# Operands at one residue of 256 bytes, and another order at the end of an output projection

## The chip, the core and the metric

The kernel runs on one core of a Trainium2 chip. The core has a matrix engine (TensorE, PE in the profile, with a second row PEld for its weight loads), a vector engine (VectorE, DVE), an activation engine (ScalarE, ACT), a general engine (GpSimd, POOL) and an engine that issues transfers (SyncE, SP). Data lie in SBUF, 128 partitions with one address range per partition, and matrix products land in PSUM. The metric is the device time of one execution in microseconds (us), as the median of several runs.

## The reference

One decoder layer on 1024 tokens of width 1024, all in float32. Two mixers work on the same normalized input, a gated DeltaNet (GDN) with 4 heads of 128 in chunks, and a native sparse attention (NSA) with 8 heads of 64 in 2 groups; their outputs are merged by gates and projected, and a SwiGLU feed-forward network (FFN, hidden width 2816) follows.

```python
h = rms_norm(x, mix_norm_gain)
qkv, z, beta, alpha, q, six K/V of NSA, gates, merge_a, merge_b = split(h @ w_in)
A = gated_delta_net(silu(causal_conv4(qkv)), beta, alpha) * gain * silu(z)
N = native_sparse_attention(q, compressed, selected and window K/V, gates)
merged = sigmoid(merge_a) * (A @ w_branch_gdn) + sigmoid(merge_b) * (N @ w_branch_nsa)
x = x + merged @ w_out
h2 = rms_norm(x, ffn_norm_gain)
gate, up = split(h2 @ w_gate_up)
x = x + (silu(gate) * up) @ w_down
out = rms_norm(x, final_norm_gain)
```

## The kernel before

**Matrix products.** Every large product runs as three matmuls per block (`mmk`, lines 143 to 145): each operand is split into a high part and a remainder by `split` (ScalarE rounds, line 81; DVE subtracts, line 82), and high x high, high x remainder and remainder x high are summed in PSUM. A matmul has a moving operand (here 512, 264 or 256 columns) and a stationary one of 128 columns, which is loaded into the array by PEld. In the timeline's name `pq<-h,whi` the moving operand stands first.

**Stages.** The input is normalized (`rms_scale`, line 156: Square on ScalarE, a scaling on DVE, a power on POOL), transposed and kept as h0 (tokens 0 to 511) and h1 (512 to 1023). Then follow the z projection (8 token tiles, a piece of 264 and a piece of 256 columns), the convolution stage (12 feature tiles; for each one product with h0, then one with h1, 8 blocks of three matmuls each), the chunk loop of GDN, woven by a planner with the projections of NSA (three pieces of 264 and two of 256 columns) and the merge gates (16 feature tiles for each half of the tokens), the attention (also woven with the gates of the second half), the branch products (32 groups of 12 matmuls), the output projection, the FFN and the down projection. In the FFN one level of a Strassen scheme is used: sums and differences of quarters of the activations (called B11, B21, B3 to B7) and of the weights (`quarters`, `left`) go into seven products instead of eight. PE's order is the order of the program; in the chunk loop and in the attention that order comes from `weave`, which asks a model of each stream which of them is ready first. Nothing of the planner's numbers belongs to the change.

**Where tiles lie.** Pools take addresses from the left in the order in which they are opened; some open at the right end (h1, later x1, and the large slots of the branch products, the output projection and the FFN). The constant pool `cp` (line 49) is the first on the left. Small tiles of odd sizes in it and in the pools behind it shift what follows. In the kernel before, the addresses of the main operands have these remainders modulo 256 bytes:

| tiles | address modulo 256 |
|---|---|
| h1, x1, AT, Aop, W, all B tiles, fraw, ahi, alo, sum, act | 224 |
| whi, wlo (split weights until the branch products; stationary for 512 columns, moving for 264 and 256) | 160 |
| h0 | 96 |
| attention: qs, qt, kt | 96 |
| attention: KT, VS, KCS, VCS | 192 |
| gain, ident | 160, 128 |
| c (FFN accumulators), xt of the down projection | 32 |
| zz, th (staging) | 32 and 64 |
| GDN tiles | 0, 32 or 160 |

**End of the output projection.** The product has two column halves. For the second, `o_last(t)` runs token tile t: 8 blocks of three matmuls (two groups kk of four k, `o_mm`), then `o_add` adds the result to x (DVE, line 1298). `h2_scale(i)` starts the norm of tile i (Square on ScalarE, a DVE operation on the sum, a power on POOL, line 162). `h2_rows(i)` finishes it on DVE (line 1329). For i = 4 to 7, `h2_sums(i, ...)` forms the sums number 5, 7, 6 and 4 of the Strassen scheme from tile i and tile i-4, by `psub` on POOL (line 88). `h2_turn(i, n, ...)` transposes such a sum on PE (four 128x128 transposes into one PSUM slot `dn`, of which there are two) and splits it into the B tiles. The argument `then` of `o_last` is a list of calls placed after k = 0, 1, 2, ... of the first group. `prepare(f, n)` splits a quarter of a gate or up weight tile; `product(f, n)` is one Strassen product of 12 matmuls; `f_sums(f)` forms the weight sums on POOL; `f_load(f)` puts the weight loads on SP's queue. From `o_last(4)` on, the order on DVE, ScalarE and POOL is the order of the program too (`manual_schedule`, line 1439), so each call stands in three queues at the place where it is written. For tile 5, for example, the lines are `o_last(5, ...)`, `h2_rows(4)`, `h2_scale(5)`, `h2_sums(4, (5, 7, 6, 4))`: the norm of tile 4 stands on DVE behind the add of tile 5, and the sums of tile 4 stand on POOL behind the power of tile 5.

**GDN tiles.** For each of 8 chunks `prepare_chunks` loads the decay sums E from DRAM (SP), takes sb = exp(E) on ScalarE (line 508), masks E on POOL (lines 510 and 512), multiplies KQ by sb on POOL, copies the last column of sb into `glast` (line 569, DVE), multiplies the products A and qkT by E on DVE (lines 581 and 582), sends A out (SP) and loads blocks of it back as U for a solve of 15 steps on DVE (lines 592 and 594). E and sb have one buffer each, `glast` three. `scan_chunks` has a tile r (DVE) and a tile vn (ScalarE); the product Y r is read into vn.

## Time and profile before

| | before |
|---|---|
| time, median of three runs | 1831.64 us (1830.16 to 1835.03) |
| profiled execution: its own time | 1833.01 us |
| its span in the trace | 1831.3 us |
| PE busy | 1736.3 us, 95% of the span |
| DVE, ACT, POOL busy | 1116.4, 768.0 and 732.7 us |
| mean granted clock of PE over the span | 0.988 of full speed |

All times of the trace count from the start of its span. A row of a timeline tells when an instruction began, how long it took, on which engine and line, out <- in by tile name, the shape, and in brackets how long the engine had been idle before it and which instruction ended that. Matmuls overlap in the pipeline, so the distance between two starts tells more than the duration of one. A granted clock of 1.00 is 2.4 GHz on PE.

### The profile page before, as it was taken

To read this page: it belongs to the slowest core of one execution; us is meant where nothing else is said; L and a number is where in the kernel's file an instruction comes from. 1 tells how busy PE (TensorE), PEld (TensorE's weight loads), DVE (VectorE), ACT (ScalarE), POOL (GpSimd) and SP (SyncE) were. 2 spreads that over 40 slices of the span, in tenths; PEclk is the share of its full clock that TensorE was granted. 3 is DMA by queue.
4 is the path that set the end of the run, shared out by engine and by line. 5 is a ranking of instruction groups with operands and counts; after the bars stand their busy time and mean duration, and the time that the engine had idled before them with its cause. 6 is when DMAs were issued, how large, how long until landed. Compare 5 with 4: busy or idle time off the path is not lost. (4 is left out here: it accounts for less than half of the span.)

```text
span 1831.3 us, 26131 instructions
## 1 busy us (share of the span) xinstructions
PE 1736.3 (95%) x9348; PEld 1459.3 (80%) x9348; DVE 1116.4 (61%) x2014; ACT 768.0 (42%) x1814; POOL 732.7 (40%) x1086
## 2 busy tenths in 40 slices
PE   7999989989999899999999998799999999989998
PEld 7888878988878777877778887588888888867776
DVE  6566466665443687776734434465655556678985
ACT  5244333343221797877722212333333333334352
POOL 3401143353231886665430301544354343354720
PEclk9999999999999999999999999899999999999999
DMA  6322443452463311111077340043233332662242
GB/s 204 98 93 93 140 118 105 107 133 66 135 187 90 94 42 47 25 47 35 13 213 215 105 166 1 19 125 99 92 118 105 106 98 92 220 234 90 83 137 99
DMA packets 183010, 196.40 MB, mean 107 GB/s; under 512 B 23408, under 2 KB 139360, under 8 KB 182880
## 3 DMA queue, kind: packets, MB, share of 16 engines
q1 hardware_dynamic: 164112, 162.03, 29.0%
q0 software_dynamic: 18560, 32.62, 5.9%
q8 instruction: 73, 1.20, 0.3%
q14 instruction: 57, 0.47, 0.1%
q10 hardware_dynamic: 208, 0.09, 0.0%
HBM read 139.01 MB, written 55.69 MB: 106 GB/s over the span
## 5 line engine op out<-in xcount | busy, mean ns | idle before, releaser
L1075 ACT ACTIVATE Ps<-s,mx 128x384 f32<-128x384 f32 (+3 forms) x192 | 106.0, 560 | 23.5 <-DVE mx L1074 22.3
L82 DVE TENSOR_TENSOR ptl<-ppt,pth 128x512 fp32r<-128x512 f32 (+1 forms) x148 | 98.9, 682 | 26.3 <-ACT pth L81 25.7
L81 ACT ACTIVATE ahi<-fraw 128x512 fp32r<-128x512 f32 x88 | 55.5, 632 | 141.4 <-PE M L144 141.4
L1105 POOL TENSOR_SCALAR Ps<-Ps,cs 128x384 f32<-128x384 f32 (+3 forms) x192 | 106.4, 571 | 13.4 <-DVE cs L1083 5.6
L1074 DVE TENSOR_REDUCE mx<-s 128x1 f32<-128x384 f32 (+3 forms) x192 | 94.8, 513 | 19.5 <-PE s L1073 14.0
L1070 PE MATMUL s<-KT,qt 128*128 128x384 f32 (+3 forms) x384 | 100.4, 362 | 2.9 <-DVE ptl L82 1.8
L143 PE MATMUL pn<-whi,h 128*128 128x264 f32 (+1 forms) x320 | 100.2, 313 | 1.4 <-ACT nst L706 1.4
L81 ACT ACTIVATE pth<-ppt 128x512 fp32r<-128x512 f32 (+1 forms) x148 | 87.1, 604 | 26.4 <-PE ppt L1128 24.1
L143 PE MATMUL pm<-h,whi 128*128 128x512 f32 x224 | 97.5, 435 | 0.2 <-ACT thm L721 0.2
L144 PE MATMUL M<-act,ahi 128*128 128x512 f32 x194 | 78.5, 404 | 13.5 <-DVE act L82 13.5
L144 PE MATMUL pn<-wlo,h 128*128 128x264 f32 (+1 forms) x320 | 91.1, 285 | 0.0
L145 PE MATMUL pn<-whi,h 128*128 128x264 f32 (+1 forms) x320 | 91.0, 284 | 0.0
L144 PE MATMUL pm<-h,whi 128*128 128x512 f32 x224 | 89.3, 399 | 0.0
L145 PE MATMUL pm<-h,wlo 128*128 128x512 f32 x224 | 89.1, 398 | 0.0
L81 ACT ACTIVATE ahi<-fsum 128x512 fp32r<-128x512 f32 x66 | 41.7, 632 | 108.3 <-PE M L144 106.8
L82 DVE TENSOR_TENSOR wlo<-wraw,whi 128x1024 fp32r<-128x1024 f32 (+1 forms) x50 | 61.1, 1231 | 41.7 <-ACT whi L81 40.0
L82 DVE TENSOR_TENSOR alo<-fraw,ahi 128x512 fp32r<-128x512 f32 x88 | 70.1, 798 | 23.8 <-ACT ahi L81 23.8
L82 DVE TENSOR_TENSOR alo<-ar,ahi 128x512 fp32r<-128x512 f32 x66 | 68.2, 1033 | 26.6 <-ACT ahi L81 26.6
L81 ACT ACTIVATE ahi<-ar 128x512 fp32r<-128x512 f32 x66 | 41.6, 630 | 101.0 <-PE dn L144 50.8
L1128 PE MATMUL ppt<-ident,Ps 128*128 128x128 f32 x528 | 77.7, 274 | 0.5 <-DVE ptl L82 0.3
L145 PE MATMUL M<-act,alo 128*128 128x512 f32 x194 | 76.7, 395 | 0.0
L143 PE MATMUL M<-act,ahi 128*128 128x512 f32 x194 | 76.0, 392 | 0.0
(506 smaller groups left out, 5569.8 us busy)
## 6 DMA issues: line engine op xcount, KB each, us to landing
wraw<-in_w_in_dram SPq DMA_DIRECT2D x50, 512.0 KB, 4.3
fraw<-in_w_gate_up_dram SPq DMA_DIRECT2D x44, 512.0 KB, 4.2
ar<-act_d SPq DMA_DIRECT2D x35, 512.0 KB, 3.5
act_d<-asum SPq DMA_DIRECT2D x44, 256.0 KB, 2.4
act_d<-act SPq DMA_DIRECT2D x33, 256.0 KB, 2.0
gt_d<-thm POOLq DMA_DIRECT2D x32, 256.0 KB, 2.9
gg<-gt_d SPq DMA_DIRECT2D x32, 256.0 KB, 2.8
qkv_d<-ac POOLq DMA_DIRECT2D x24, 256.0 KB, 2.3
```

Of the source, the lines that this page charges most:

```text
L81: nc.scalar.activation(hi, src, AF.Copy)
L82: nc.vector.tensor_tensor(lo, src, hi.bitcast(F32), op=ALU.subtract)
L143: nc.tensor.matmul(ps, ah, bh, start=first, stop=False)
L144: nc.tensor.matmul(ps, ah, bl, start=False, stop=False)
L145: nc.tensor.matmul(ps, al, bh, start=False, stop=last)
L1070: nc.tensor.matmul(s, qt[:, h, l, :], KT[g][:, b, j0 * P + c0:j0 * P + c1], start=l == 0, stop=l == 1 and not ext)
L1074: nc.vector.tensor_reduce(mx[:, h, n:n + 1], s, axis=AX.X, op=ALU.max, negate=True)
L1075: nc.scalar.activation(pr, s, AF.Exp, bias=mx[:, h, n:n + 1], accum_out=sums[:, h, n:n + 1])
L1105: nc.gpsimd.tensor_scalar(v, v, cs[:, h, n:n + 1], 1.0, op0=ALU.mult, op1=ALU.mult)
L1128: nc.tensor.transpose(pt[:k, h, :], prs[h][:, jj * P:jj * P + k], ident)
```

## The change

First, tiles move and grow so that main operands have the remainder 224 modulo 256 bytes. Two unused tiles of 24 and 48 columns are put into the constant pool, and `expo` becomes a slice of a tile of 64 columns; the small statistics of the norms (`rms_ss`, `rms_r`, `rms_ss2`, `rms_ms`) move to the constant pool; `wraw`, `zz`, `nst`, `convw`, `rr`, `so`, `ro`, `rowvis` and `mx` become wider than what is used of them; r and vn of GDN share one buffer; and `glast` is allocated, and copied, behind the transfer of A instead of ahead of the products A and qkT.

Second, the end of the output projection gets another order. `then` becomes a table from k (0 to 7, over both groups) to calls. The two turns of a tile stand after k = 1 and after k = 3 instead of both after one k. From tile 5 on, the norm of the tile before (`h2_rows`) and its sums 5 and 7 stand amid the next tile's matmuls, ahead of that tile's power in POOL's queue; sums 6 and 4 follow behind `h2_scale`. `prepare(0, 1)` and `prepare(0, 2)` move into tile 7, `h2_turn(4, 6)` goes ahead of `h2_rows(7)`, the sums 5 and 7 of tile 7 go to DVE (`vsub`), and `prepare(1, 1)` goes ahead of `h2_turn(7, 3, 7)`.

```diff
...
+    cp.tile([P, 24], F32, tag="pad", name="pad")
...
-    expo = cp.tile([P, 8], F32, tag="expo", name="expo")
+    small = cp.tile([P, 64], F32, tag="small", name="small")
+    expo = small[:, 0:8]
...
+    cp.tile([P, 48], F32, tag="pad2", name="pad2")
...
-            raw = wp.tile([P, 4, cols], F32, tag="wraw", name="wraw", bufs=3)
+            raw = wp.tile([P, 4, 272 if cols > 256 else cols], F32, tag="wraw", name="wraw", bufs=3)[:, :, :cols]
...
-        ss = p.tile([P, 1], F32, tag="rms_ss", name="rms_ss", bufs=2)
+        ss = cp.tile([P, 1], F32, tag="rms_ss", name="rms_ss", bufs=2)
...
-            zz = sp.tile([P, 256], F32, tag="zz", name="zz", bufs=2)
+            zz = sp.tile([P, 320], F32, tag="zz", name="zz", bufs=2)[:, :256]
...
-            glast = gt("glast", [P, H], 3)
-            nc.vector.tensor_copy(glast, sb[:, :, P - 1])
             yield 230, 1200
...
             nc.sync.dma_start(square(sq_a[c % 2]), A)
             U = gt("U", [32, 16, 16])
+            glast = gt("glast", [P, H], 3)
+            nc.vector.tensor_copy(glast, sb[:, :, P - 1])
             nc.sync.dma_start(U, blocks(sq_a[c % 2]))
...
-                r = gt("r", [P, H, P])
+                r = gt("rv", [P, H, P])
...
-            vn = gt("vn", [P, H, P])
+            vn = gt("rv", [P, H, P])
...
-            for g in then[k:k + 1]:
+            for g in then.get(k + (0 if first else 4), ()):
                 g()
...
-    def h2_sums(i, which):
+    def h2_sums(i, *which, sub=psub):
...
-        o_last(4, [lambda: None, partial(h2_turn, 2, 1, 2)])
+        o_last(4, {1: [partial(h2_turn, 2, 1)], 3: [partial(h2_turn, 2, 2)]})
         h2_scale(4)
-        o_last(5, [lambda: None, partial(h2_turn, 3, 1, 2)])
-        h2_rows(4)
+        o_last(5, {1: [partial(h2_turn, 3, 1)], 3: [partial(h2_rows, 4), partial(h2_sums, 4, 5, 7), partial(h2_turn, 3, 2)]})
         h2_scale(5)
-        h2_sums(4, (5, 7, 6, 4))
-        o_last(6, [lambda: None, lambda: None, partial(h2_turn, 4, 3, 7)])
-        h2_rows(5)
+        h2_sums(4, 6, 4)
+        o_last(6, {1: [partial(h2_turn, 4, 3)], 3: [partial(h2_rows, 5), partial(h2_sums, 5, 5, 7), partial(h2_turn, 4, 7)]})
         h2_scale(6)
-        h2_sums(5, (5, 7, 6, 4))
-        o_last(7, [lambda: None, lambda: None, partial(h2_turn, 5, 3, 7)])
-        h2_rows(6)
+        h2_sums(5, 6, 4)
+        o_last(7, {1: [partial(h2_turn, 5, 3)], 3: [partial(h2_rows, 6), partial(h2_sums, 6, 5, 7), partial(h2_turn, 5, 7)],
+                   5: [partial(prepare, 0, 1)], 6: [partial(prepare, 0, 2)]})
         h2_scale(7)
-        prepare(0, 1)
-        h2_sums(6, (5, 7))
         f_sums(0)
-        prepare(0, 2)
         h2_turn(6, 3, 7)
         early[0, 1] = product(0, 1)
+        h2_turn(4, 6)
         h2_rows(7)
-        h2_turn(4, 6)
         h2_turn(5, 6)
-        h2_sums(7, (5,))
-        h2_sums(6, (6,))
-        h2_sums(7, (6, 7))
+        h2_sums(7, 5, 7, sub=vsub)
+        h2_sums(6, 6)
+        h2_sums(7, 6)
         f_load(1)
         early[0, 2] = product(0, 2)
+        prepare(1, 1)
         h2_turn(7, 3, 7)
-        prepare(1, 1)
         early[1, 1] = product(1, 1)
...
```

## Rows read from the trace of the kernel before

**Rows 1.** The page: busy time, share of the span and instructions of each engine.

```profile
PE 1736.3 (95%) x9348; PEld 1459.3 (80%) x9348; DVE 1116.4 (61%) x2014; ACT 768.0 (42%) x1814; POOL 732.7 (40%) x1086
```

**Rows 2.** Stretches: length, busy PE, PEld, DVE, ACT, POOL (instructions), clock, DMA.

```profile
65.00:205.00 140.00, 140.00 (x637) 115.12 (x636) 83.29 (x118) 53.76 (x85) 17.15 (x31) 1.00 0.28 92
...
1116.00:1181.00 65.00, 48.23 (x211) 37.34 (x209) 26.76 (x39) 20.55 (x36) 31.02 (x27) 0.89 0.03 9
1181.00:1632.00 451.00, 451.00 (x2006) 373.39 (x2005) 273.77 (x391) 156.42 (x259) 183.81 (x133) 1.00 0.41 131
```

**Rows 3.** Timeline of PE: matmuls 24 apart in gapless runs of three stages.

```profile
93.98 0.39 PE L143 MATMUL pq<-h,whi 128*128 128x512 f32 x1
...
99.57 0.39 PE L143 MATMUL pq<-h,whi 128*128 128x512 f32 x1
...
105.07 0.39 PE L143 MATMUL pq<-h,whi 128*128 128x512 f32 x1
...
999.78 0.39 PE L144 MATMUL M<-AT,whi 128*128 128x512 f32 x1
...
1005.27 0.39 PE L144 MATMUL M<-h,whi 128*128 128x512 f32 x1
...
1239.67 0.39 PE L143 MATMUL M<-B7h,ahi 128*128 128x512 f32 x1
...
1245.11 0.39 PE L143 MATMUL M<-B5h,ahi 128*128 128x512 f32 x1
```

**Rows 4.** Timeline of PE at the end of the output projection, 1116 to 1182.

```profile
1115.98 0.48 PE L143 MATMUL M<-W,Aop 128*128 128x512 f32 x1
...
1120.32 0.66 PE L1357 MATMUL dn<-ident,row 128*128 128x128 f32 x4 [2.27 <-DVE B21l L82]
...
1136.96 1.12 PE L1357 MATMUL dn<-ident,xt 128*128 128x128 f32 x4 [2.78 <-POOL xt L88]
...
1177.70 0.50 PE L143 MATMUL M<-B21h,ahi 128*128 128x512 f32 x1 [1.25 <-ACT ahi L81]
...
1181.02 1.03 PE L1357 MATMUL dn<-ident,row 128*128 128x128 f32 x8
```

**Rows 5.** Timelines of DVE and POOL in the same stretch, by engine.

```profile
1118.38 1.28 DVE L1329 SCALAR_TENSOR_TENSOR row<-x,rms_r,fgain 128x1024 f32<-128x1024 f32 x1 [0.73 <-POOL rms_r L162]
...
1131.52 0.69 DVE L1298 SCALAR_TENSOR_TENSOR x<-M,x 128x512 f32<-128x512 f32 x1 [2.64 <-PE M L145]
1132.13 1.28 DVE L1329 SCALAR_TENSOR_TENSOR xt<-x,rms_r,fgain 128x1024 f32<-128x1024 f32 x1
...
1117.79 0.55 POOL L162 TENSOR_TENSOR rms_r<-rms_ss,expo 128x1 f32<-128x1 f32 x1 [5.79 <-DVE rms_ss L160]
...
1133.78 0.55 POOL L162 TENSOR_TENSOR rms_r<-rms_ss,expo 128x1 f32<-128x1 f32 x1 [5.82 <-DVE rms_ss L160]
1134.30 1.27 POOL L88 TENSOR_TENSOR row<-xt,row 128x512 f32<-128x512 f32 x1
```

**Rows 6.** As rows 2, behind three gaps: the longest stretch and the sum.

```profile
1157.00:1163.80 6.80, 5.79 (x16) 4.73 (x17) 2.32 (x3) 0.60 (x1) 6.64 (x5) 0.50 0.01 2
...
sum 13.50, PE 11.77 PEld 9.30 DVE 4.36 ACT 3.31 POOL 10.36; mean PE 3.92 PEld 3.10 DVE 1.45 ACT 1.10 POOL 3.45
```

**Rows 7.** Groups of DVE instructions by line and shape: busy us, mean ns.

```profile
L1501 DVE TENSOR_TENSOR c<-M,c 128x512 f32<-128x512 f32 x22 | 15.2, 691 | 30.6 <-PE M L145 30.6
```

**Rows 8.** Timelines of DVE and POOL at 1154.

```profile
1154.47 2.37 DVE L82 TENSOR_TENSOR alo<-fraw,ahi 128x512 fp32r<-128x512 f32 x2 [0.36 <-ACT ahi L81]
...
1154.71 1.58 POOL L88 TENSOR_TENSOR row<-xt,row 128x512 f32<-128x512 f32 x1
```

**Rows 9.** The tile glast (ns min/median/max; who waited), and ScalarE's timeline.

```profile
L569 DVE COPY glast<-sb x8: 147/162/164, 225.1 to 425.3; 128x4 f32<-128x4 f32 x8
...
  POOL E L510: 4.2, 1
...
326.38 0.63 ACT L508 ACTIVATE sb<-E 128x512 f32<-128x512 f32 x1 [3.52 <-DMA E<-gc_d]
```

More of the change, by code (lines that the diff above doesn't have):

```diff
@@ L156, in rms_scale @@
     def rms_scale(p, src, nfeat, junk):
-        ss = p.tile([P, 1], F32, tag="rms_ss", name="rms_ss", bufs=2)
+        ss = cp.tile([P, 1], F32, tag="rms_ss", name="rms_ss", bufs=2)
         nc.scalar.activation(junk, src, AF.Square, accum_out=ss)
         nc.vector.tensor_scalar(ss, ss, 1.0 / nfeat, EPS, op0=ALU.mult, op1=ALU.add)
-        r = p.tile([P, 1], F32, tag="rms_r", name="rms_r", bufs=2)
+        r = cp.tile([P, 1], F32, tag="rms_r", name="rms_r", bufs=2)
         nc.gpsimd.tensor_tensor(r, ss, expo[:, 0:1], op=ALU.pow)
@@ L297, in tile_hybrid @@
     ogain = cst.tile([P, P], F32, tag="ogain", name="ogain")
-    convw = cst.tile([P, 4, 12], F32, tag="convw", name="convw")
+    convw = cst.tile([P, 64], F32, tag="convw", name="convw")[:, :48].rearrange("p (t f) -> p t f", t=4)
     ba = cst.tile([P, NT, 8], F32, tag="ba", name="ba")
@@ L361, in tile_hybrid @@
         nc.tensor.transpose(pc[:, 0, :48], cw[:48, :], ident[:48, :48])
-        nc.vector.tensor_copy(convw.rearrange("p t f -> p (t f)"), pc[:, 0, :48])
+        nc.vector.tensor_copy(convw, pc[:, 0, :48].rearrange("p (t f) -> p t f", t=4))
         wz = piece()
@@ L535, in prepare_chunks @@
             nc.vector.scalar_tensor_tensor(ss, ss, 4 * EPS, rscale, op0=ALU.add, op1=ALU.mult)
-            rr = gt("rr", [P, 8], 2)
+            rr = gt("rr", [P, 24], 2)[:, :8]
             nc.gpsimd.tensor_tensor(rr, ss, expo, op=ALU.pow)
@@ L666, in scan_chunks @@
                 Sst = Sn
-            so = gt("so", [P, H], 2)
+            so = gt("so", [P, 16], 2)[:, :H]
             jo = gt("jk", [P, P])
@@ L672, in scan_chunks @@
             nc.vector.tensor_scalar(so, so, 4.0 / P, 4 * EPS, op0=ALU.mult, op1=ALU.add)
-            ro = gt("ro", [P, H], 2)
+            ro = gt("ro", [P, 16], 2)[:, :H]
             nc.gpsimd.tensor_tensor(ro, so, expo[:, 0:4], op=ALU.pow)
@@ L704, in projections @@
                 yield from mm3g(pt[:, :n], hT(i), lambda k: (wh[:, k, :], wl[:, k, :]), KD, 110)
-                st = sp.tile([P, 264], F32, tag="zz", name="nst", bufs=2)
+                st = sp.tile([P, 320], F32, tag="zz", name="nst", bufs=2)
                 nc.scalar.copy(st[:, :n], pt[:, :n])
@@ L761, in tile_hybrid @@
         nc.vector.tensor_copy(mask, mtmp)
-    rowvis = kvt("rowvis", [P, 1])
+    rowvis = kvt("rowvis", [P, 64])[:, 0:1]
     nc.vector.memset(rowvis, 1.0)
@@ L1028, in scores @@
                 cs = at_("cs", [P, 4, 2], 4)
-                mx = at_("mx", [P, 4, 2], 4)
+                mx = at_("mx", [P, 4, 4], 4)[:, :, :2]
                 gv = ga[:, :, br]
@@ L1285, in tile_hybrid, with o_mm @@
         w_ops(1, kk, hl, lambda: f_raw("wops").rearrange("p (m k) t -> p m (k t)", m=2))
-    def o_mm(bank, t, c, kk, first, last, then=()):
+    def o_mm(bank, t, c, kk, first, last, then={}):
         n, sl = t // 4, slice(t % 4 * P, t % 4 * P + P)
@@ L1306, in tile_hybrid, with o_last @@
                     o_add(t0 + t, 0, banks[t])
-    def o_last(t, then=()):
+    def o_last(t, then={}):
         bank = psF("M")
@@ L1311, in o_last @@
         for kk in order:
-            o_mm(bank, t, 1, kk, kk == order[0], kk == order[1], then if kk == order[0] else ())
+            o_mm(bank, t, 1, kk, kk == order[0], kk == order[1], then)
         o_add(t, 1, bank)
@@ L1337, in h2_sums @@
             if n == 5:
-                psub(b11, b12, b11)
+                sub(b11, b12, b11)
             elif n == 7:
-                psub(b12, b22, b12)
+                sub(b12, b22, b12)
             elif n == 6:
                 t2 = tt.tile([P, 512], F32, tag="t2", name="t2", bufs=2)
-                psub(t2, b22, b11)
+                sub(t2, b22, b11)
                 turned[i, 6] = t2
             elif n == 4:
-                psub(b21, b21, turned[i, 6])
+                sub(b21, b21, turned[i, 6])
         turned.update({(i, n): {5: b11, 7: b12, 4: b21, 3: b22}[n] for n in (*which, 3) if n != 6})
@@ L1604, in square_sum @@
         if i not in sums:
-            sums[i] = xp.tile([P, 2], F32, tag="rms_ss2", name="rms_ss2", bufs=4)
+            sums[i] = cp.tile([P, 2], F32, tag="rms_ss2", name="rms_ss2", bufs=4)
         nc.scalar.activation(part("sq", "xt")[:, 0], x1[i][:, c * 512:c * 512 + 512], AF.Square, scale=D ** -0.5,
@@ L1609, in final @@
     def final(i):
-        ms = xp.tile([P, 1], F32, tag="rms_ms", name="rms_ms", bufs=2)
+        ms = cp.tile([P, 1], F32, tag="rms_ms", name="rms_ms", bufs=2)
         nc.vector.tensor_scalar(ms, sums[i][:, 0:1], sums[i][:, 1:2], EPS, op0=ALU.add, op1=ALU.add)
-        r = xp.tile([P, 1], F32, tag="rms_r", name="rms_r", bufs=2)
+        r = cp.tile([P, 1], F32, tag="rms_r", name="rms_r", bufs=2)
         nc.gpsimd.tensor_tensor(r, ms, expo[:, 0:1], op=ALU.pow)
```

4 lines of the change are left out of this document (2 added, 2 removed).

## The prediction, made blind

> **What bounds the kernel now.** I read the page's busy line first [rows 1]: TensorE (PE) is busy for 1736.3 of 1831.3 us, so the question is where its stream of matmuls could be denser. The table by stretches [rows 2] answers that for stages: in the convolution stretch (65 to 205) and in the FFN (1181 to 1632) PE has no gap at all, while at the end of the output projection (1116 to 1181) it is busy for 48.23 of 65 us and the granted clock is 0.89 of 2.4 GHz. So two kinds of time can be won: spacing inside a gapless stream, and gaps in one stretch of 65 us.
>
> For the spacing I took start times of matmuls 24 apart, all 128x512, in three gapless runs [rows 3]. Convolution, first half of the sequence: 93.98 to 99.57, 5.59 us, 232.9 ns each. Second half of the same piece: 99.57 to 105.07, 229.2 ns. Branch products: 999.78 to 1005.27, 228.8 ns. FFN: 1239.67 to 1245.11, 226.7 ns. Same shape, same full clock, three prices. What differs is where the operands lie (the table of residues above): moving 96 and stationary 160, moving 224 and stationary 160 (twice), both 224. The convolution pair is the best evidence, since only the moving half changes within one loop.
>
> For the gaps I read PE's timeline in the stretch [rows 4], then the chain behind one gap on the other engines [rows 5], then the clock [rows 6].
>
> **Alignment: sum.** After the change the small tiles of the norms stand in the constant pool: 96 + 512 + 256 + 192 bytes, then 64 + 64 + 128 + 64 for the statistics, 1376 in all from 16,512, so the pools start at 17,888, residue 224, the residue at which the right-hand side of SBUF already lies. A wraw buffer becomes 4352 bytes, zz 1280, convw 256, rowvis 256, the small GDN tiles fill multiples of 256: everything that PE reads in these stages stands at 224. Exceptions: the 264-column pieces, whose moving slices still step by 1056 bytes; they gain nothing. Nothing is added to a queue by this. For the other engines I count 0: adds whose tile c lies at residue 32 take 691 ns [rows 7], the add into x at residue 224 0.69 us [rows 5].
> - At 96 against 160: 288 convolution and 384 gate matmuls (first half), 672 x 6.2 ns = 4.2 us.
> - At 224 against 160: 288 convolution, 384 gate (second half) and 384 branch matmuls, 1056 x 2.3 ns = 2.4 us.
> - Attention (scores 192 against 96, products 224 against 192): 648 matmuls worth 552 of 512 columns. No gapless run of 24 exists there, so bounds: 0, and 552 x 6.2 = 3.4 us. I take 1.5, since PE also waits on other engines in that stretch.
> - 576 matmuls of 256 columns: bounds 0 and half the price of 512, 576 x 3.1 = 1.8. I take 1.0.
> - Output projection, FFN and down projection are at 224 against 224 already: 0.
> Sum 9.1 us, taken as 9; ends 0 and 11.8.
>
> The Trainium skill speaks against this part: "SBUF — State Buffer", section "Who interferes with whom", gives TensorE two independent read ports and states that PE and ACT never wait on anyone. By that rule operand addresses cannot matter and this part is worth 0. The 6.2 ns between two halves of one loop [rows 3] are not explained by it, so I keep the 9 us and carry the rule as a rival.
>
> **Reordering: what stands there.** Output tile t = 4 to 7 has 24 matmuls (5.44 us at 226.7 ns) and two turns of four transposes. Before, tile i's sums run only after the next tile is finished: x(5), the add of tile 5, at 1131.52, then the norm of tile 4 on DVE (1132.13, 1.28 us), behind it on POOL first the power of tile 5 (1133.78), then two subtractions (from 1134.30, 1.34 us each), and PE, which has come to the turn of the second, starts it at 1136.96 after 2.78 us [rows 4, 5]. The same wait comes back in the next two tiles. Between the first (2.27 at 1120.32) and the last (1.25 at 1177.70) there are eight gaps, 16.5 us in all [rows 4]. After three of them the granted clock is 0.50, the lower level of 1.2 GHz, for 13.5 us in all, the longest piece 6.8 us [rows 6]; half of 13.5, some 6.8 us, is lost there. Full check: from 1115.98, the start of tile 4, to 1181.02 [rows 4] are 65.0 us; 144 matmuls and 64 transposes (0.10 us each) need 39.0; the excess is 26.0, of which gaps and clock explain 23.3.
>
> **Reordering: the new schedule**, on the old clock, with DVE 0.69 per add or split and 1.28 per norm, POOL 0.55 per power and 1.34 per subtraction, and the chain delays of [rows 5]: from the start of the add to that of the power 2.26 (1131.52 to 1133.78, the square on ScalarE between them), from power to norm 0.59 (1117.79 to 1118.38).
> Tile 4 starts at 1115.98. Its first turn now takes six matmuls, then six more, then the second turn, which still waits for DVE's split, as PE does now until 1120.32 [rows 4]: gap 1.0 instead of 2.27. Tile 4 ends at 1123.5, power at 1126.0, norm(4) 1126.9 to 1128.2, subtractions 1128.2 to 1130.8, ahead of power(5) (1132.4) in POOL's queue. Tile 5 ends at 1130.0. Tile 6: its second turn comes at 1133.2, after 1130.8: no gap; ends 1136.4. POOL meanwhile does (4;6,4) to 1135.6 and (5;5,7) to 1138.2, power(6) 1138.9, (5;6,4) to 1142.1. Tile 7: second turn at 1139.6, no gap; ends 1142.9. Here POOL is late: (6;5,7) end at 1144.7 and the turn of (6,7) waits 1.5. Product (0,1) then ends at 1148.0, turn (4,6), (5,6), product (0,2) ends at 1151.6; turn (7,7) needs the DVE subtractions behind norm(7) (1149.9 to 1151.2) and B6l: 1153.0, gap 1.1. Product (1,1) ends at 1156.3, turns, then product (1,2) waits for its split as before and ends at 1161.9. Against 1181.02 that is 19.1 us less, with no gap above 1.5 until the last (1.25 before) and so probably no half clock.
>
> What it moves: the norms and subtractions go ahead of the powers on POOL, so each power waits behind up to two subtractions (2.6 us); DVE's norm and split wait for the power, and ScalarE's next split for nothing. POOL's work per tile is 0.55 + 4 x 1.34 = 5.9 us against PE's 6.4: it is nearly the bound. The two splits prepare(0,1), (0,2) move into tile 7 ahead of x(7): 2 x 0.69 on DVE, up to 1.2 us late. SP's second load of f = 1 waits only for f_sums(0), which now ends at 1151 instead of 1164.05, so it is earlier. Extra cost to subtract: DVE operations with two SBUF inputs and POOL's stretch each other, 2.37 us for two splits and 1.58 for the subtraction beside them [rows 8]. Ten POOL subtractions and two DVE ones at +0.3 each, half of it on the path: 1.5 to 2. Taken: 17; ends 12 (all of the stretching, and one half-clock window of 3.4 us at half loss) and 19.
>
> **GDN.** The glast copy moves behind the decay products on DVE. r and vn share one slot, which costs nothing: vn is written only after the product that reads r. For glast the cover is the reload of E, which can start only when those products have read E: ScalarE waits 3.52 us for it before it rewrites sb at 326.38 [rows 9], and the copy takes 0.16. Cost 0; end below 0: A is earlier by one copy in each of 8 chunks, 1.3 us; above: rival E.
>
> **Sum.** The profiled execution took 1833.0 us (span 1831.3), 1.4 above the median. 1831.6 - 9 - 17 = 1805.6; I write 1805.5.
>
> **Rivals.**
> - B: residues don't set the spacing; the two halves differ by something else, or the layout comes out other than I worked out. Only the reordering pays: 1831.6 - 17 = 1814.6. For: spacing alone names no cause. Against: the two halves of one loop. 14%.
> - C: POOL becomes the bound. At 1.58 per subtraction its tile takes 6.9 us, over PE's 6.4; gaps return at each second turn, the clock drops in two windows. Reordering pays 9, total 1831.6 - 18 = 1813.6. For: [rows 8]. Against: DVE has few two-input operations in these tiles. 12%.
> - D: the weaves of GDN and attention, whose PE order is fixed by a planner, lose what the rest wins: within 0.3%, 1831. Against: none of their instructions is added. 6%.
> - E, slower: DVE takes the glast copies behind the 15-step solve that follows. Then sb's rewrite and with it the next chunk's decay waits; a wait on such a copy was 4.2 us once [rows 9]. From 26 / 8 = 3.3 us in each of 8 chunks it eats everything; at 4.2, 33.6 are lost: 1839. Against: the 3.5 us of cover. 6%.
>
> **How the numbers follow.** A, the sum, 62%: between 1799.5 (19 + 11.8 + 1.3 for glast) and 1811 (12 + 9). The range takes A, B and C with the bound of 12 for B (1819.6): 1799 to 1820. Under about 0.3% (5.5 us) this kernel's times don't tell a change from none. Faster A + B + C = 0.88, same D 0.06, slower E 0.06.
>
> **What would show it.** Right: convolution and branch runs of 24 at 5.44 us; second turns of tiles 6 and 7 (transposes after 12 matmuls) without a gap; 1116 to 1181 shrinks to about 47 with the clock at 1.0; FFN unchanged at 226.7. Wrong: runs still at 5.59 (B), POOL subtractions of 1.6 with gaps before the turns (C), longer waits in the chunk loop (D, E).

## The result, and the profile after

The changed kernel takes 1811.06 us (median of four runs, 1808.63 to 1818.86) where the kernel before took 1833.34 beside it: a ratio of 0.9888, 95% interval 0.9868 to 0.9907, 22.3 us less. The forecast was 1805.5 in a range from 1799 to 1820, faster. The time lies in the range, 5.5 us above the forecast, at the upper end of what the forecast gave its own sum, A (1799.5 to 1811), and nearer to the sum of rival C (1813.6).

The changed kernel's page, and its stretches with the columns of [rows 2]: up to the start of output tile 4, from there to the transposes behind product (1,2), and the FFN behind them.

```profile
PE 1726.6 (95%) x9348; PEld 1456.4 (80%) x9348; DVE 1121.1 (62%) x2016; ACT 768.0 (42%) x1814; POOL 733.8 (41%) x1084
...
980.00:1105.80 125.80, 125.80 (x566) 104.33 (x564) 50.22 (x70) 25.29 (x37) 22.28 (x19) 1.00 0.39 127
1105.80:1159.10 53.30, 45.69 (x211) 36.43 (x209) 31.08 (x41) 20.54 (x36) 30.52 (x25) 0.90 0.04 11
1159.10:1632.00 472.90, 465.43 (x2050) 383.82 (x2048) 295.80 (x406) 161.16 (x267) 203.22 (x144) 0.99 0.39 125
```

Two places hold the whole difference between the two profiled executions (spans 1831.3 and 1809.4, 21.9 us apart). Tile 4 starts at 1105.78 instead of 1115.98 [rows 4]: 10.2 us. From there to the transposes behind product (1,2) it takes 53.3 us instead of 65.0: 11.7 us. What follows takes 650.3 us in both. The granted clock of that stretch is still 0.90.

First the spacing, on PE's timeline of the changed kernel: convolution, matmuls 24 apart, in the first and in the second half of the sequence.

```profile
94.03 0.39 PE L147 MATMUL pq<-h,whi 128*128 128x512 f32 x1
...
99.47 0.39 PE L147 MATMUL pq<-h,whi 128*128 128x512 f32 x1
...
104.91 0.39 PE L147 MATMUL pq<-h,whi 128*128 128x512 f32 x1
```

Both halves take 5.44 us, 226.7 ns each, where they took 5.59 and 5.50 [rows 3]. Then the end of the output projection, PE's timeline from the start of tile 4:

```profile
1105.78 0.47 PE L147 MATMUL M<-W,Aop 128*128 128x512 f32 x1
...
1110.12 0.66 PE L1361 MATMUL dn<-ident,row 128*128 128x128 f32 x4 [0.88 <-DVE B21l L86]
...
1129.32 0.60 PE L1361 MATMUL dn<-ident,xt 128*128 128x128 f32 x4
...
1136.18 1.12 PE L1361 MATMUL dn<-ident,xt 128*128 128x128 f32 x4 [3.07 <-POOL xt L92]
...
1148.56 0.88 PE L1361 MATMUL dn<-ident,xt 128*128 128x128 f32 x4 [2.23 <-DVE xt L95]
...
1155.79 0.50 PE L147 MATMUL M<-B21h,ahi 128*128 128x512 f32 x1 [1.25 <-ACT ahi L85]
...
1159.11 1.04 PE L1361 MATMUL dn<-ident,row 128*128 128x128 f32 x8
```

The gaps before the turns of tiles 4 and 5 are gone (the second turn in tile 7, at 1129.32, starts without one), but one of 3.07 us stands at the second turn of tile 6 and one of 2.23 at that of tile 7. What DVE and POOL did before the first of them:

```profile
1116.62 1.28 DVE L1333 SCALAR_TENSOR_TENSOR xt<-x,rms_r,fgain 128x1024 f32<-128x1024 f32 x1
...
1129.38 2.25 DVE L1333 SCALAR_TENSOR_TENSOR xt<-x,rms_r,fgain 128x1024 f32<-128x1024 f32 x1
...
1132.16 2.84 DVE L86 TENSOR_TENSOR alo<-fraw,ahi 128x512 fp32r<-128x512 f32 x2
...
1130.63 2.15 POOL L92 TENSOR_TENSOR row<-row,t 128x512 f32<-128x512 f32 x1
1132.75 1.71 POOL L92 TENSOR_TENSOR row<-xt,row 128x512 f32<-128x512 f32 x1
1134.53 1.59 POOL L92 TENSOR_TENSOR xt<-xt 128x512 f32<-128x512 f32 x1
```

The norm of tile 4 (1116.62), with POOL idle, takes 1.28 us. The norm of tile 6 (1129.38) runs beside sums 6 and 4 of tile 5 and takes 2.25, the second of these subtractions 2.15. Only then come the two that PE waits for, beside the splits of the first weight tile (two in 2.84 us, from 1132.16), at 1.71 and 1.59. And behind the gap the clock falls:

```profile
1135.10:1141.90 6.80, 5.72 (x16) 4.67 (x17) 1.96 (x4) 2.23 (x4) 5.67 (x6) 0.50 0.01 2
...
1136.95 0.78 PE L147 MATMUL M<-B11h,ahi 128*128 128x512 f32 x1
...
1142.11 1.03 PE L1361 MATMUL dn<-ident,t 128*128 128x128 f32 x8
1142.90 0.47 PE L147 MATMUL M<-B21h,ahi 128*128 128x512 f32 x1
```

In it lies product (0,1). From its first matmul (1136.95) to the next transposes (1142.11) it takes 5.16 us; product (0,2), as many matmuls at full clock, takes 2.84 (1142.90 to the next transposes at 1145.74).

### The profile page after: what moved, and what is told of

It is laid out like the page before. It is cut to its first block, busy times and chain, and to the rows that moved or that the text cites. A ratio compares the mean times of both kernels' runs of the same rounds, so it can differ in the third digit from the quotient of the medians.

```text
span 1809.4 us, 26138 instructions
## 1 busy us (share of the span) xinstructions
PE 1726.6 (95%) x9348; PEld 1456.4 (80%) x9348; DVE 1121.1 (62%) x2016; ACT 768.0 (42%) x1814; POOL 733.8 (41%) x1084
## 5 line engine op out<-in xcount | busy, mean ns | idle before, releaser
L1079 ACT ACTIVATE Ps<-s,mx 128x384 f32<-128x384 f32 (+3 forms) x192 | 106.0, 560 | 23.6 <-DVE mx L1078 22.6
L85 ACT ACTIVATE pth<-ppt 128x512 fp32r<-128x512 f32 (+1 forms) x148 | 87.1, 604 | 25.3 <-PE ppt L1132 24.6
L86 DVE TENSOR_TENSOR alo<-ar,ahi 128x512 fp32r<-128x512 f32 x66 | 68.1, 1032 | 26.6 <-ACT ahi L85 26.6
```

What stands on the lines that cost most here:

```text
L85: nc.scalar.activation(hi, src, AF.Copy)
L86: nc.vector.tensor_tensor(lo, src, hi.bitcast(F32), op=ALU.subtract)
L1079: nc.scalar.activation(pr, s, AF.Exp, bias=mx[:, h, n:n + 1], accum_out=sums[:, h, n:n + 1])
```

## The experiments

My theory after the result: the two parts add up; the residues are the cause of the first; the second lost 5 us to POOL's and DVE's queues at two turns and to the half clock behind them. "The stretch" below is always the one from the start of output tile 4 to the transposes behind product (1,2): 65.04 us before, 53.33 in the changed kernel.

### The alignment alone

```diff
...
+    cp.tile([P, 24], F32, tag="pad", name="pad")
...
+    cp.tile([P, 48], F32, tag="pad2", name="pad2")
...
-            raw = wp.tile([P, 4, cols], F32, tag="wraw", name="wraw", bufs=3)
+            raw = wp.tile([P, 4, 272 if cols > 256 else cols], F32, tag="wraw", name="wraw", bufs=3)[:, :, :cols]
...
```

(and the rest of the first part; the end of the output projection is that of the kernel before)

> The alignment alone (tiles moved, widened and shared, the copy of glast moved), the end of the output projection as before. My theory: the two parts are independent, and everything that the changed kernel gained ahead of output tile 4 (its start moved from 1115.98 to 1105.78, 10.2 us) belongs to this part: span about 1821.1, time about 1821.5, tile 4 starts near 1105.8, and the stretch from there to the transposes behind product (1,2) keeps its 65.0 us. Rival 1: the gain ahead of tile 4 is shared with the other part through changed buffers or queues: then the start of tile 4 lies between 1107 and 1116. Rival 2: the end stretch became shorter because its own operands moved: then it takes less than 65 us here.

Measured: 1828.15 us against 1834.44 beside it, ratio 0.997 (0.9957 to 0.9983): 3.1 to 7.9 us, less than the 10 expected. In its trace the convolution has 226.7 ns in both halves. Tile 4 starts at 1109.4, and the stretch has the old gaps, the longest as long as before:

```profile
1109.41 0.47 PE L147 MATMUL M<-W,Aop 128*128 128x512 f32 x1
...
1113.75 0.66 PE L1361 MATMUL dn<-ident,row 128*128 128x128 f32 x4 [2.27 <-DVE B21l L86]
...
1153.09 1.12 PE L1361 MATMUL dn<-ident,xt 128*128 128x128 f32 x4 [3.36 <-POOL xt L92]
...
1176.16 1.04 PE L1361 MATMUL dn<-ident,row 128*128 128x128 f32 x8
```

The stretch takes 66.8 us, 1.7 more than before: behind the first gap (2.27, the same as in [rows 4]) the clock fell here for 3.4 us, and there it did not. So rival 2 falls. Of the 10.2 us ahead of tile 4 this execution shows 6.6. The half clock may explain part: its total ahead of tile 4 is 20.5 us here and before, but 13.6 in the profile of the changed kernel, and 6.9 us at half speed can be worth up to 3.4 us. It does not explain all: the next run has 27.3 us of it ahead of tile 4 and starts tile 4 earlier than the kernel before. Rival 1 is not needed; the start of tile 4 lies between 1107 and 1116 as it said, but the next runs, which have the layout and the new order, scatter in the same way, and the convolution and the stretch from the banks M to tile 4 take the same here as in the changed kernel (130.6 and 175.9 us).

### The new order alone

```diff
...
-            for g in then[k:k + 1]:
+            for g in then.get(k + (0 if first else 4), ()):
                 g()
...
```

(and the rest of the second part; every tile lies where it was)

> The new order at the end of the output projection alone, with every tile where it was before. My theory: 11.7 us less (65.0 to 53.3 between the start of tile 4 and the transposes behind product (1,2)), nothing elsewhere: span about 1819.6, time about 1819.9; convolution runs of 24 matmuls stay at 5.59 and 5.50 us. The gap of about 3 us at the second turn of tile 6 and the half clock behind it stand here too. Rival: the stretched norms and subtractions on DVE and POOL come from tiles that moved; then the gap is gone here and the stretch takes about 48 us.

Measured: 1819.82 us against 1834.44, ratio 0.9921 (0.9903 to 0.9939), 14.6 us less, in its interval 11.2 to 17.8. PE's timeline:

```profile
1115.07 0.48 PE L143 MATMUL M<-W,Aop 128*128 128x512 f32 x1
...
1145.56 1.12 PE L1357 MATMUL dn<-ident,xt 128*128 128x128 f32 x4 [3.11 <-POOL xt L88]
...
1168.40 1.03 PE L1357 MATMUL dn<-ident,row 128*128 128x128 f32 x8
```

1115.07 to 1168.40 are 53.33 us, to the hundredth what the changed kernel has, with the same gap. The convolution keeps 231.0 ns in the mean of both halves. The rival (moved tiles stretch DVE and POOL) falls. That the two stretches are equal is partly chance: the half clock behind the first gap lasts 3.4 us here and 6.8 in the changed kernel, and here PE waits longer afterwards (2.76 us instead of 2.23 at the second turn of tile 7, and 0.49 for a split behind it). The two parts add up: 6.3 and 14.6 are 20.9, measured together 22.3 and, in a second comparison, 22.6.

### Matmuls alone, over a grid of residues

```python
for c, n in enumerate((512, 256)):
    for s in range(8):
        for m in range(8):
            for k in range(8):
                nc.tensor.matmul(b, st[s][:, 0, :], mv[m][:, 0, :n], ...)
                nc.tensor.matmul(b, st[s][:, 0, :], mv[m][:, 1, :n], ...)
                nc.tensor.matmul(b, st[s][:, 1, :], mv[m][:, 0, :n], ...)
```

> The disputed cost by itself: no layer is computed, only matmuls on tiles at chosen addresses. Eight moving tiles and eight stationary tiles lie at the residues 0, 32, ..., 224 modulo 256; each of the 64 pairs runs 24 matmuls (high, high, remainder of the stationary tile, as in the kernel), first with 512 columns, then with 256. My theory: the distance between the residues of moving and stationary decides, so the table is constant along diagonals: 226.7 ns per matmul of 512 columns at distance 0, about 233 at moving minus stationary = -64, about 229 at +64; for 256 columns the other way round, since the changed kernel shows 119.0 ns at distance 0 where the kernel before shows 116.4 at -64 and +64. Rival 1, the residue of one operand decides (rows or columns of the table are constant). Rival 2, addresses don't matter: one value per size, 226.7 and 113.4 to 119, and what the kernel gained has another cause, such as other engines' traffic.

Measured, mean distance of two starts in ns (rows: residue of the moving tile, columns: of the stationary one):

```
512 columns      128    160    192    224      0     32     64     96
moving 128     226.8  233.0  233.1  234.3  233.5  233.2  228.7  233.3
       160     233.4  227.7  233.1  233.0  234.1  232.3  233.7  228.7
       192     229.3  233.4  227.7  233.0  233.5  233.9  233.1  233.9
       224     233.9  229.3  233.5  226.9  233.1  233.3  234.2  233.5
         0     233.5  233.9  229.3  233.4  227.7  233.1  233.0  234.0
        32     234.0  233.5  233.9  229.3  233.4  227.7  233.0  233.5
        64     233.5  234.0  233.5  233.9  229.3  233.4  226.9  233.0
        96     233.1  233.5  234.0  233.5  233.9  229.3  233.4  227.7
256 columns      128    160    192    224      0     32     64     96
moving 128     119.3  118.3  117.8  118.6  118.4  120.0  117.8  117.7
       160     118.0  119.7  118.3  117.6  117.3  119.1  119.8  117.8
       192     118.0  118.0  119.7  118.3  114.7  117.4  118.8  120.0
       224     119.6  118.0  118.0  119.7  118.0  113.7  117.4  118.3
         0     118.7  119.6  118.0  118.0  119.7  118.0  117.7  117.3
        32     117.4  118.7  119.6  118.0  118.0  119.7  118.2  114.7
        64     113.7  117.4  118.7  119.6  118.0  118.0  119.7  118.0
        96     118.0  113.7  117.4  118.7  119.6  118.0  118.0  119.7
```

The rows behind five of these cells, first and last of 24 matmuls each; the letter stands for the residue (m moving, s stationary; b is 160, d is 224, h is 96):

```profile
118.52 0.40 PE L45 MATMUL b<-md,sb 128*128 128x512 f32 x1
...
123.80 0.39 PE L47 MATMUL b<-md,sb 128*128 128x512 f32 x1
...
140.86 0.40 PE L45 MATMUL b<-mh,sb 128*128 128x512 f32 x1
...
146.23 0.39 PE L47 MATMUL b<-mh,sb 128*128 128x512 f32 x1
...
207.85 0.40 PE L45 MATMUL b<-md,sd 128*128 128x512 f32 x1
...
213.07 0.39 PE L47 MATMUL b<-md,sd 128*128 128x512 f32 x1
...
484.78 0.28 PE L45 MATMUL b<-mb,sd 128*128 128x256 f32 x1
...
487.48 0.28 PE L47 MATMUL b<-mb,sd 128*128 128x256 f32 x1
...
490.44 0.28 PE L45 MATMUL b<-md,sd 128*128 128x256 f32 x1
...
493.19 0.28 PE L47 MATMUL b<-md,sd 128*128 128x256 f32 x1
```

23 distances each: 5.37 us (233.5 ns) at (96, 160), 5.28 (229.3 in the table, from unrounded times) at (224, 160), 5.22 (226.9) at (224, 224); for 256 columns 2.70 at (160, 224) and 2.75 at (224, 224). These are the three prices of [rows 3], in a program in which no other engine works beside PE. The tables are nearly constant along diagonals: for 512 columns the distance of the two residues sets the price, 227 at 0, 229 at moving minus stationary = 64, 232 to 234 at all others. Both rivals fall, and with them rival B of the prediction. For 256 columns equality is no best case: 119.7 ns on nearly the whole diagonal, 113.7 to 117.8 at -64. There the distance alone does not decide (at -64 there are cells of 113.7 to 114.7 and of 117.6 to 117.8); why was not looked into.

### Tile 5's sums late

```diff
...
         h2_scale(6)
-        h2_sums(5, 6, 4)
         o_last(7, {1: [partial(h2_turn, 5, 3)], 3: [partial(h2_rows, 6), partial(h2_sums, 6, 5, 7), partial(h2_turn, 5, 7)],
                    5: [partial(prepare, 0, 1)], 6: [partial(prepare, 0, 2)]})
+        h2_sums(5, 6, 4)
         h2_scale(7)
...
```

> The changed kernel with one move: sums 6 and 4 of tile 5 stand on POOL behind sums 5 and 7 of tile 6 instead of ahead of them. My theory: the 3.07 us gap at the second turn of tile 6 comes from POOL's queue, which runs sums 6 and 4 of tile 5 beside the norm of tile 6, so that both are stretched (norm 2.25 us, subtraction 2.15), and only then starts the sums that PE waits for. Then the norm of tile 6 takes 1.28 us here, the gap is at most 1.2 us, the 6.8 us of half clock behind it are gone, and the stretch from tile 4 to the transposes behind product (1,2) takes 48 to 50 us instead of 53.33. Rival 1: the splits of the first weight tile, which stretch the two sums to 1.71 and 1.59 us, make the gap: then it stays above 2 us. Rival 2: the wait only moves on to the turn of sum 6 of tile 5: then that turn waits 2 us or more and the stretch stays above 52 us.

DVE's norm of tile 6, then PE's timeline (it begins tile 4 at 1105.36):

```profile
1128.96 1.27 DVE L1333 SCALAR_TENSOR_TENSOR xt<-x,rms_r,fgain 128x1024 f32<-128x1024 f32 x1
...
1133.39 0.66 PE L1361 MATMUL dn<-ident,xt 128*128 128x128 f32 x4 [0.69 <-POOL xt L92]
...
1153.86 1.03 PE L1361 MATMUL dn<-ident,row 128*128 128x128 f32 x8
```

The norm takes 1.27 instead of 2.25 us, the gap is 0.69 instead of 3.07, there is no half clock in the stretch, and it takes 48.50 us: 4.8 less, as the theory had it. Where the sums of tile 5 now stand, the next wait is 0.70 us, at the turn of sum 6 of tile 4, and a split on DVE ends it. Both rivals fall. The second gap stays (2.26 us at the last turn of tile 7), here without half clock behind it. One execution: 1806.54 us.

### Tile 7's norm early

```diff
...
         early[0, 1] = product(0, 1)
-        h2_turn(4, 6)
         h2_rows(7)
-        h2_turn(5, 6)
         h2_sums(7, 5, 7, sub=vsub)
+        h2_turn(4, 6)
+        h2_turn(5, 6)
...
```

> The changed kernel with the norm of tile 7 and its two DVE subtractions ahead of the turns of sum 6 of tiles 4 and 5 in DVE's queue. My theory: the second gap (2.23 us at the last turn of tile 7) is DVE's queue: the norm of tile 7 waits behind a split that needs PE to end product (0,1) first. With the norm and the subtractions in DVE's idle time from 1138.6 to 1143.3 the gap and the 3.4 us of half clock behind it are gone: 3 to 4 us less in the stretch, 49.3 to 50.5 us. Rival: beside POOL's four weight sums the norm and the subtractions are stretched to 2.2 us and more each, so the split of sum 6 comes late and product (0,2) waits: then the stretch gains under 1.5 us.

```profile
1146.49 0.66 PE L1361 MATMUL dn<-ident,xt 128*128 128x128 f32 x4 [3.09 <-POOL xt L92]
...
1154.95 1.03 PE L1361 MATMUL dn<-ident,xt 128*128 128x128 f32 x8
...
1150.33 1.65 DVE L95 TENSOR_TENSOR row<-xt,row 128x512 f32<-128x512 f32 x1
```

The second gap is gone: the transposes of tile 7 start at 1154.95 without a wait, although the subtractions are stretched to 1.65 us (the rival had 2.2 and more). The stretch takes 48.11 us, 5.2 less, more than expected: behind the first gap, of the same 3.09 us, the half clock lasted 3.4 us here and 6.8 in the changed kernel. The whole execution is long all the same (1816.3): ahead of tile 4 it has 34.1 us of half clock, in code that the move does not touch, and tile 4 starts at 1116.1.

### The weight splits put back

```diff
...
-        o_last(7, {1: [partial(h2_turn, 5, 3)], 3: [partial(h2_rows, 6), partial(h2_sums, 6, 5, 7), partial(h2_turn, 5, 7)],
-                   5: [partial(prepare, 0, 1)], 6: [partial(prepare, 0, 2)]})
+        o_last(7, {1: [partial(h2_turn, 5, 3)], 3: [partial(h2_rows, 6), partial(h2_sums, 6, 5, 7), partial(h2_turn, 5, 7)]})
         h2_scale(7)
+        prepare(0, 1)
         f_sums(0)
+        prepare(0, 2)
...
```

> The changed kernel with the two splits of the first weight tile put back behind the add and the start of the norm of tile 7, where the kernel before had them. If rival 1 of the run with tile 5's sums moved holds (these splits make the gap), the gap at the second turn of tile 6 falls from 3.07 to under 1 us and the stretch takes 50 us or less. My theory: the two subtractions there shrink from 1.71 and 1.59 to about 1.3 us, 0.7 us together, so the gap is still 2.3 us or more, and product (0,1) begins no earlier, because it waits for its split: the stretch stays within 1 us of 53.3 or gets longer.

```profile
1135.96 0.66 PE L1361 MATMUL dn<-ident,xt 128*128 128x128 f32 x4 [2.32 <-POOL xt L92]
```

The two subtractions take 1.26 and 1.27 us and the gap is 2.32, so the splits account for 0.75 of the 3.07; most of the rest is POOL's queue, as the run with tile 5's sums late showed. The stretch takes 51.68 us, 1.65 less and outside of "within 1 us": behind this gap the clock did not fall. It fell once later, for 3.4 us, behind the gap at tile 7, which is 3.01 us here. One execution: 1810.03 us.

### Three moves, then four

The two moves above that helped, and the split for product (1,2) ahead of the turns before it:

```diff
...
+        prepare(1, 2)
         h2_turn(6, 6)
         h2_turn(7, 6)
-        prepare(1, 2)
...
```

> Three moves together: tile 5's sums 6 and 4 late, tile 7's norm and subtractions early, and the split for product (1,2) ahead of the two turns of sum 6 before it (in the changed kernel product (1,2) starts 1.25 us late for that split). My theory: no gap above 1.2 us and no half clock between tile 4 and the transposes behind product (1,2); the stretch takes 43 to 46 us (144 matmuls at 226.7 ns and 64 transposes are 39.0 us at full clock), and the kernel is 7 to 10 us faster than the changed one, near 1802. Rival: the moves compete for the same POOL and DVE time and the sum is below 4 us.

```profile
1144.36 1.26 PE L1361 MATMUL dn<-ident,xt 128*128 128x128 f32 x8 [1.84 <-DVE B6l L86]
```

No half clock, the stretch 46.37 us, a little above the expected 43 to 46, since a gap of 1.84 remains: DVE's split of sum 6 stands behind subtractions that take 1.67 and 1.65 us beside POOL's weight sums. 1807.03 us (1805.11 to 1814.22), ratio 0.9877 (0.9847 to 0.9908) to the kernel before beside it, 25.3 us less, where the changed kernel had 22.3 less (0.9868 to 0.9907): 3 us more where 7 to 10 were expected, and not clear of the noise. So the trace shows the gain in the stretch, and the time does not exclude the rival's "below 4 us".

So the next one gives tile 7's sums back to POOL and puts the weight sums behind them:

```diff
...
-        f_sums(0)
         h2_turn(6, 3, 7)
         early[0, 1] = product(0, 1)
         h2_rows(7)
-        h2_sums(7, 5, 7, sub=vsub)
         h2_turn(4, 6)
         h2_turn(5, 6)
+        h2_sums(7, 5, 7)
         h2_sums(6, 6)
         h2_sums(7, 6)
+        f_sums(0)
         f_load(1)
...
```

> The kernel of the run with three moves, and one more: the two sums 5 and 7 of tile 7 go back to POOL, and POOL's four weight sums of the first weight tile stand behind them and behind the sums 6 of tiles 6 and 7. My theory: in the run with three moves the last large gap (1.84 us at the last turns of tile 7) comes from DVE, where norm and subtractions run beside the weight sums at 1.42, 1.67 and 1.65 us; without these beside it the norm takes 1.28, POOL's sums are done when PE comes, the gap is under 0.7 us and the stretch takes 44 to 45.5 us instead of 46.37. Rival: POOL's queue is now the bound, a gap of 1 us or more stands before a turn of sum 6 or before product (0,6), and the stretch is no shorter.

The stretch takes 43.86 us with no gap above 0.9. What follows takes 651.65 us, 1.3 more than in the changed kernel; 1.1 of them are there after 12 us, with gaps of 0.48 and 0.24 us before turns that wait for nothing in the changed kernel. That is part of the rival, behind the stretch instead of in it. One execution: 1805.76 us.

### The 256-column pieces elsewhere

```diff
...
-        hi = wp.tile([P, 8, cols], F32R, tag="whi", name="whi", bufs=2)
+        hi = wp.tile([P, 2112], F32R, tag="whi", name="whi", bufs=2)[:, off:off + 8 * cols].rearrange("p (k c) -> p k c", k=8)
...
-    want([(0, 8, 0, 256, wcols(w_in, 1536, 1792))], 256)
+    want([(0, 8, 0, 256, wcols(w_in, 1536, 1792))], 256, False, 48)
...
```

> The changed kernel with the split weights of the three pieces of 256 columns at the residue 160 instead of 224 (the stationary tiles h0 and h1 stay at 224). My theory: with 256 columns equal residues are a slow case; the table of the run on matmuls alone gives 119.7 ns at (224, 224) and 117.6 at moving 160 and stationary 224. Then the mean spacing of the 256-column matmuls falls from 119.8 and 119.0 (z projection, projections of NSA) by about 2 ns, 576 x 2.1 = 1.2 us, which is too little to be seen in the time of one execution; everything else keeps its spacing. Rival: in the kernel the spacing of these matmuls is set by what else runs, and stays at 119.

The z projection, 45 distances of matmuls of 256 columns, in the changed kernel:

```profile
63.16 0.28 PE L149 MATMUL pz<-whi,h 128*128 128x256 f32 x1
...
68.56 0.28 PE L149 MATMUL pz<-whi,h 128*128 128x256 f32 x1
```

and with these pieces at residue 160:

```profile
63.53 0.29 PE L149 MATMUL pz<-whi,h 128*128 128x256 f32 x1
...
68.64 0.28 PE L149 MATMUL pz<-whi,h 128*128 128x256 f32 x1
```

5.40 us become 5.11, 120.0 ns become 113.6; in the projections of NSA 119.0 become 116.1. That is 3 to 6 ns, more than expected; the addresses do set the spacing here, but the grid's prices do not carry over: it has 117.6 for this pair, and the same 45 distances take 5.30 us in the kernel before and 5.10 in the run with the new order alone, whose tiles lie alike. So the rival falls only in part. In the time of one execution (1811.49) the move can't be seen, nor in the length of the stage: from the first matmul of the z projection to the convolution it takes 60.3 us, and 60.0 to 61.3 with these pieces at 224.

### All moves, beside the changed kernel

> Both together: the order of the run with the weight sums behind tile 7's sums, and the 256-column pieces at residue 160. My theory: 8 to 10 us from the stretch and about 1 from the spacing against the changed kernel, so 1800 to 1803 us where the changed kernel has 1811; the difference between the two is clear of the noise on one chip. Rival: the number of half-clock stretches elsewhere in an execution differs more than that, and the two intervals overlap.

> The changed kernel itself, once more, on the same chip as the run with all moves: the measure for it. I expect 1811 us, a stretch of 53.3 us in the trace, and a number of half-clock stretches ahead of output tile 4 that may differ from the 3 of its first profile, while the stretch itself repeats.

Measured on one chip: all moves 1803.34 us (1801.13 to 1805.69), ratio 0.9838 (0.982 to 0.9857) to the kernel before; the changed kernel 1810.28 (1808.0 to 1813.12), ratio 0.9874 (0.9855 to 0.9893). The times don't overlap; the two intervals overlap by 0.0002. So this version is about 7 us faster than the changed kernel, a little under the 8 to 10 expected. Its stretch and its turn of tile 7:

```profile
1105.80:1149.70 43.90, 41.24 (x212) 33.35 (x211) 28.14 (x39) 20.58 (x36) 26.82 (x23) 1.00 0.00 1
...
1142.81 0.66 PE L1361 MATMUL dn<-ident,xt 128*128 128x128 f32 x4 [0.35 <-POOL xt L92]
```

The clock of the stretch is 1.00, 41.24 of 43.90 us are busy. The changed kernel's second profile has 53.34 us there and the same two gaps (3.09 and 2.21), and 17.1 us of half clock ahead of tile 4 instead of 13.6. So the stretch repeats here (in the run with the 256-column pieces, with the same order, it takes 54.29) and the clock elsewhere does not, as expected.

## Why the prediction was right, and where it was off

**Spacing: right in its mechanism, too large in its sum.** The mechanism (distance of residues) was argued from two halves of one loop and is now shown by the grid and by the alignment alone. The convolution gave 2.5 us (133.1 to 130.6 from its first matmul to the next stage, in all ten profiles with the new layout); the terms of the sum say 288 x 6.2 + 288 x 2.3 = 2.4. From the first matmul into the banks M (the last gates, then the branch products) to tile 4 it is 1.1 us (176.9 to 175.9); the forecast's price for these 96 gate and 384 branch matmuls is 480 x 2.3 = 1.1. From the first gate matmul (tile pm) to the tile ppos of the attention, with 228 gate matmuls of the first half, it is about 2 (82.4 and 83.0 with the old layout, 80.3 to 80.7 in nine of the ten new profiles); 228 x 6.2 = 1.4 were forecast. None of these stretches has half clock in it (0.1 us at most).

**The rule of the Trainium skill.** "SBUF — State Buffer", section "Who interferes with whom", would have made this part 0, as the prediction read it. The grid differs from that: with no other engine at work a matmul of 512 columns takes 226.8 to 234.3 ns by the addresses of its own two operands. The measurement decides here; what the page states of PE against other engines was not tried.

**Three smaller terms of it: off.** 576 matmuls of 256 columns were booked as a gain of 1.0 us with bounds 0 and 1.8. The sign was wrong: they went from 117.8 and 116.4 to 119.9 and 119.0 ns, a loss of 192 x 2.1 + 384 x 2.6 = 1.4 us in spacing (the stage of the z projection did not get longer by it: 60.7 us before, 60.4 after). The price of 512 columns was carried over to a shape for which the trace had no pair to compare, and a loss was not among the bounds. The woven gates came from 233 to 229 ns in the median, instead of to the 226.7 of a gapless run; why is open. For the attention (1.5 booked) the stretch from the first transposes of K to the banks M is 333.6 and 334.1 us with the old layout and 331.3 to 333.4 in nine of the ten profiles with the new one (338.4 in the tenth, with 17.1 us of half clock). Most of that is the clock: the kernel before has 3.4 us of half clock near 853 (and as much near 611), and the four new profiles that have it too, at 845 to 848, take 333.2 to 333.4; the five with 331.3 to 331.6 have none. Like with like it is 0.4 us at most, with the gates of the second half in it: little of the 1.5 is left.

Together: forecast 9, timed alone 6.3 (3.1 to 7.9), so the 9 lies outside. Of the 10.2 us between the two first profiles, 5.5 stand in the three stretches without half clock. Another 1.8 stand between ppos and the first transposes of K, where the kernel before, the order alone and the alignment alone have 6.8 us of half clock and take 69.7 to 69.9 us, and eight of the ten new profiles have 3.4 and take 68.1 to 68.2. The loop has 2.2, and scatters as much within the new layout. Whether the layout has a part in these last two is open.

**Reordering up to tile 7: right to 0.2 us.** With tile 4 set to 1115.98 the forecast had the second turn of tile 6 at 1133.2, that of tile 7 at 1139.6 and tile 7's end at 1142.9; the trace, 10.2 us earlier throughout, has 1133.1, 1139.5 and 1142.7, and the gap in tile 4 at 0.88 instead of 1.0.

**Reordering behind tile 7: the step that was mis-sized.** The prediction took 17 us (12 to 19); by the traces it is 11.7, by the times of the order alone 14.6 (11.2 to 17.8). Two terms failed. The gap at (6,7) was put at 1.5 us and is 3.07, that at (7,7) at 1.1 and is 2.23: 2.7 us. The stretching was known [rows 8], but booked as 0.3 us per operation, half on the path; ahead of (6,7) all that fell to POOL's queue was on the path. The subtraction beside the norm of tile 6 took 0.9 more than the 1.29 of one alone, and the two behind it, which PE waited for, 0.4 and 0.3 more: together the 1.6 that this gap was too long. The norm took 0.97 more too, but ended (1131.63) before POOL came free (1132.75). The run with tile 5's sums late shows that this order makes the gap, the run with the weight splits put back that 0.75 of it are theirs. And from the small gaps followed "probably no half clock": there are 10.2 us of it in the stretch, up to 5.1 us lost (2.3 of them in product (0,1)). The schedule had the stretch at 45.9 us, and it is 53.33: of the 7.4 more, 2.7 are the two gaps and the half clock can be the rest. How much each cost by itself is open, since they are not independent: the order alone has 3.4 us less half clock, a longer wait at (7,7), and the same 53.33.

**Rivals.** C (POOL becomes the bound, gaps at each second turn, two stretches of half clock, 1813.6) describes the end of the stretch and comes within 2.6 us of the result, but by one turn on POOL and one on DVE, not by each tile, and its terms (9 for each part) are not those that were measured: that its sum is so near is in part luck. It deserved more than 12%. B falls with the grid. D and E are not seen: from the first projection of NSA to the gates the loop takes 247.7 and 246.3 us with the old tiles and 245.4 to 247.8 with the new, so the copy of glast costs nothing there that can be measured, where E had 26 us and more; POOL's mask waited for it 14.9 us in two chunks, and the loop was no longer for it.

**Sum.** 9 + 17 forecast; about 6 to 10 and 11.7 by the traces, 6.3 and 14.6 by the times, 22.3 together. By the times both parts gave less than was taken, 26 in all; the range was wide enough for it.

## What to carry to other kernels

Price a shape by rows of that shape: what a residue did to 512 columns said nothing of 256. When a chain is moved ahead in a queue, write down what runs beside each of its links on the other engine (here DVE and POOL stretched each other), and book the whole stretched duration of every link in the queue that the wait ends on. A gap of 2 to 3 us on PE should be priced with the half clock that may follow it: in the changed kernel's stretch up to 5.1 us, beside 7.6 us of gaps.

## What the runs showed of the hardware

For 512 columns, a matmul whose two operands lie at the same residue of 256 bytes starts every 227 to 228 ns, with moving minus stationary = 64 every 229, else every 232 to 234; for 256 columns the same residue is a slow case (119.7 against 113.7 at best).

The same gap does not always bring the clock down from 2.4 to 1.2 GHz: behind 3.07 to 3.11 us at the same turn the half clock lasted 6.8 us in two executions and 3.4 us in three others, and behind 2.32 it did not fall. At the last turn of tile 7 it fell for 3.4 us behind 2.23 us in the changed kernel, and not behind 2.26 in the run with tile 5's sums late. Ahead of tile 4 the total of half clock ranged from 6.8 to 34.1 us among executions of nearly the same code, and the start of tile 4, with the same tiles, from 1105.4 to 1116.1; but the totals do not order the starts (6.8 us goes with 1106.3, 13.6 with 1105.8). A single profile is therefore good for the length of a gapless stretch without half clock (130.6 us for the convolution and 175.9 from the banks M to tile 4 in all ten profiles with the new layout), and poor for a whole time: the four of the changed kernel lie up to 10 us apart.
